# Weight low parts by an accumulating transfer, ten seven-product forms ahead, and two rounds instead of three in the down projection of a trunk layer

## The chip, the cores and the metric

The kernel runs on one core of a Trainium2 chip. The core has five engines with instruction queues of their own: PE (matrix products), DVE and ACT (elementwise work), POOL, and SP, which here issues the transfers between HBM and the on-chip memory. The metric is the device time of one execution in microseconds (us), the median of several runs.

## The reference

One layer works on 128 context tokens and 512 latent tokens (640 together), model width 1024. A mixer stage (mLSTM, convolution, merge, `wo`) comes first. The change lies in the second half, the gated MLP:

```
h2 = rmsnorm(x, p['norm2_g']) * (1 + sc2) + sh2
gate, val = jnp.split(jnp.einsum('btd,df->btf', h2, p['w_up']), 2, axis=-1)
gate = dwconv_grid(gate, p['ffn_dw_w'], p['ffn_dw_b'])      # 3x3 (latent), width 3 (context)
x = x + g2 * jnp.einsum('btf,fd->btd', jax.nn.gelu(gate) * val, p['w_down'])
y = rmsnorm(x, final_norm_g)
```

The inner width is 2816, which is 22 tiles of 128 ("f tiles"). The scale `g2` comes from a linear map of the conditioning vector.

## The kernel before

**Precision.** Every operand of a product is split into a high part and a low part (`hi` is the value rounded to fp32r, `lo` is the value minus `hi`). `three` (line 566) issues three products for each block: high by high, high weight by low data, low weight by high data. So the low part of a weight is read by the third matmul of its block.

**Weights.** All weight blocks of 128x128 stand in HBM in the order in which they are used, eight to a group (512 KB). `load` (436) has SP fetch a group into one of three stage tiles `wst`. `prep` (449) makes `wh` (ACT, a rounding copy) and `wl` (DVE, `tensor_sub` of `wst` and `wh`). There are three `wh` and three `wl` tiles (`NWT`), so `ahead` (518), called when a group begins, prepares the group two places on, whose tiles the group just finished has released.

**The MLP.** `ffn_tile(f)` (1536) computes the gate half of tile f (eight blocks, two column halves of 320 tokens, three products: 48 matmuls) and the value half (another 48). `ffn_gate` copies the gate to `gbuf` on ACT, makes `acc` there, and queues eight taps (`ffn_tap`, DVE). `ffn_out` applies gelu (ACT) and multiplies by the value (DVE, `ge`).

**Rounds.** The down projection of f tiles 0 to 17 is done in three rounds of six f tiles (`ROUNDS`). A round (`dn_round`, 1572) uses a seven-product scheme on 2x2 blocks (token halves by output tiles): in each of four quarters seven products of nine matmuls each, 252 matmuls of 320 columns in place of the 288 of the plain form. Its weights are "forms" (`prep_form`, 470): three are raw blocks (A11, A12, A22), four are sums (S1 to S4, DVE, tile `sf`). Each form gets `hi` (ACT) and `lo` (DVE), both in one `wh` or one `wl` tile, so six forms can be ahead. Its data forms `xf` are made by `pair_forms` (1513) for each pair of f tiles.

Within a quarter the same PSUM bank is read between products: after A11, S2, S3 and so on, `residual` (1338) adds `gate * bank` to the stream `x`, and only then may the next product accumulate into that bank:

```
(pa, "A11", "B11", True, [(m1, 0)]),
(pb, "S1", "T1", True, [(m2, 1)]),
(pa, "S2", "T2", False, [(m1, 1)]),
(pd, "A12", "B21", True, [(m1, 0)]),
(pa, "S3", "T3", False, [(m2, 1)]),
(pb, "S4", "B22", False, [(m1, 1)]),
(pa, "A22", "T4", False, [(m2, 0)]),
```

So DVE must answer A11 while PE does S1, S2 while PE does A12, and S3 while PE does S4.

**The last f tiles.** Tiles 18 to 21 (`LASTF`) are projected in the plain way, once for tokens 0 to 383 (`dnA`) and once for tokens 384 to 639 (`dnB`), with their weight blocks fetched and split for both. For `dnA` the first three output tiles are begun with all but the last f tile. Then `final` scales the result and SP writes it out.

**Order.** Order of issue follows a planner (`_Order`, 167) that keeps estimated times for each engine. DVE's background work waits in `od.bg`: lanes below 20 are taps, lane 20 is the map of the conditioning vector (`ada_tile`, tile `junk`, source tiles `ad`). `step` takes from it while DVE's estimated time stands less than a slack past PE's: `SLACK` for taps, `self.slack` (here `SLACK_FFN`, -1000 ns) for lane 20. `od.need("g2")` in `dn_round` (1572, first round) issues all that is left of the map at that point.

Of the kernel before, what the change touches and what calls it, by code (L numbers as in the profile page):

```python
# [15 lines left out]
P = 128  # L16
# [38 lines left out]

ROUNDS = [list(range(6 * r, 6 * r + 6)) for r in range(3)]
LASTF = list(range(18, NF))
UPS = [list(range(0, 7)), list(range(7, 13)), list(range(13, 19)), list(range(19, NF))]
NPR = 3
# [106 lines left out]
class _Order:  # L166
# [7 lines left out]
    def __init__(self):  # L174
        self.free = {"Q": 1700.0}
        self.ready = {}
        self.side = []
        self.bg = {}
        self.line = None
        self.filling = False  # L180
        self.table = None
        self.hold = False
        self.slack = SLACK
        self.used = {}
        self.rings = {}
        self.avail = {}
# [38 lines left out]
    def issue(self, key, name, ops, args, kw):  # L225
        out, ins = ops[0], ops[1:]
        acc = kw.get("accum_out")
        t = max([self.free.get(key, 0.0)] + [self.ready.get(a.tensor.name, 0.0) for a in ins if a is not acc])
        if key == "Q":
            t = max(t, self.now)  # L230
        t = max(t, self.avail.pop(out.tensor.name, 0.0))
        if key in ("V", "S", "G"):
            t = max(t, self.ready.get(out.tensor.name, 0.0) - self.LAT)
        t += self.cost(key, name, ops, args, kw) * (2 if key == "PE" and t < COLD else 1)
        self.free[key] = t
        done = t + (2000.0 if key == "Q" else self.LAT)
        for a in (out,) if acc is None else (out, acc):
# [57 lines left out]
    def step(self):  # L295
        for t in list(self.side):
            if not t[2] and t[0] <= self.now:
                self._go(t)
        while self.idle_work() and self.free.get("V", 0.0) < self.now + (SLACK if min(self.bg) < 20 else self.slack):
            self.fill()  # L300
# [39 lines left out]
def tile_trunk(  # L340
# [17 lines left out]
    od = _Order()  # L358
    V, S, G, PE, Q = (_Timed(e, od, k) for e, k in ((nc.vector, "V"), (nc.scalar, "S"), (nc.gpsimd, "G"),
                                                    (nc.tensor, "PE"), (nc.sync, "Q")))  # L360

# [17 lines left out]
    ctx.enter_context(tc.manual_schedule())  # L379
    first = ExitStack()  # L380
    adp = first.enter_context(tc.tile_pool(name="adp", bufs=2 * NAD1))
# [67 lines left out]
    def prep(g):  # L449

        if g in ready or g >= NGRP:
            return
        load(g)
        src = stage.pop(g)
        hi = od.ring("wh", wp.tile([P, GB * P], F32R, tag="wh", name="wh"), NWT)
        lo = od.ring("wl", wp.tile([P, GB * P], F32R, tag="wl", name="wl"), NWT)

        def parts():
            yield from od.until(src)
            S.activation(hi, src, AF.Copy)  # L460
            yield
            V.tensor_sub(lo, src, hi.bitcast(F32))
            live.pop(g)

        ready[g] = (hi, lo)
        lines[g] = od.spawn(parts())

    sums_, form_at = {}, {}

    def prep_form(g, j):  # L470
# [9 lines left out]
        a21, a22, a11, a12 = t2[:, 0:FW_], t2[:, FW_:2 * FW_], t1[:, 0:FW_], t1[:, FW_:2 * FW_]  # L480
        tag = ("wh", "wl")[UNIT_AT[u] % 2]
        w = od.ring(tag, wp.tile([P, GB * P], F32R, tag=tag, name=tag), NWT)
        hi, lo = w[:, 0:FW_], w[:, 512:512 + FW_]
        nm = FORMS[j]

        def parts():
# [17 lines left out]
            S.activation(hi, src, AF.Copy)  # L504
            yield
            V.tensor_sub(lo, src, hi.bitcast(F32))
            for gg in (g, g + 1):
# [10 lines left out]
    def ahead(i):  # L518

        room = 2 * NWT  # L520
        while i < len(UNITS):
            kind, g, j = UNITS[i]
            room -= 2 if kind == "c" else 1
            if room < 0:
                break
            if kind == "c":
                prep(g)
# [757 lines left out]
    def close_mid():  # L1285
# [4 lines left out]
        ap2 = ctx.enter_context(tc.tile_pool(name="ap2", bufs=NA2))  # L1290
        adp2 = ctx.enter_context(tc.tile_pool(name="adp2", bufs=NAD))
        ada_cond()
# [180 lines left out]
    def ffn_out(f, pvt):  # L1473
# [11 lines left out]
        if f in LASTF:  # L1485
            hi, lo = A2([P, T], F32R, "ah"), A2([P, T], F32R, "al")
            yield
# [8 lines left out]
    xf, ges, xlive = {}, {}, [0]  # L1496

    def x_form(p, nm, src):

        if xlive[0] < (NA2 if g2_in else NA2 - 4):  # L1500
            t = A2([P, 2, TH], F32R, "xf")
            xlive[0] += 1
            xa2.append(p // 3)
        else:
            t = A([P, 2, TH], F32R, "xf")
        S.activation(t[:, 0, :], src, AF.Copy)
# [46 lines left out]

    od.slack = SLACK_FFN
    first3 = [0, NF, 1]
# [16 lines left out]
    def dn_round(r):  # L1572

        fs = ROUNDS[r]
        for f in fs:
            od.finish(t_act[f])
        if r == 0:
            od.need("g2")
            g2_in.append(True)
        for q in range(4):  # L1580
# [204 lines left out]
```

## Time and profile before

| what | value |
|---|---|
| median of three runs | 1000.87 us (1000.29 to 1001.52) |
| the profiled execution, its own time | 1001.8 us |
| its span | 999.6 us |
| granted TensorE clock, mean | 0.984 |
| busy: PE, DVE, ACT, POOL | 941.7, 803.4, 430.6, 6.0 us |
| HBM read | 105.12 MB |
| MLP begins, up products with h2 | about 489 us |
| last matmul of the down projection | 985 us |

The busy time of an engine says how much of the span it worked. The trace also gives, for each instruction, when it began, and what ended the idle time before it; the latter is what the reading below goes by. Almost every instruction carries the line of the helper that records it (L161 before, L165 after), so tiles tell them apart. A duration of an instruction on DVE or ACT overlaps the next one's beginning a little.

### The profile page before, as it was taken

To read this page: it belongs to the slowest core of one execution; us is meant where nothing else is said; L and a number is where in the kernel's file an instruction comes from. 1 tells how busy PE (TensorE), PEld (TensorE's weight loads), DVE (VectorE), ACT (ScalarE), POOL (GpSimd) and SP (SyncE) were. 2 spreads that over 40 slices of the span, in tenths; PEclk is the share of its full clock that TensorE was granted. 3 is DMA by queue.
4 is the path that set the end of the run, shared out by engine and by line. 5 is a ranking of instruction groups with operands and counts; after the bars stand their busy time and mean duration, and the time that the engine had idled before them with its cause. 6 is when DMAs were issued, how large, how long until landed. Compare 5 with 4: busy or idle time off the path is not lost.

```text
span 999.6 us, 16748 instructions
## 1 busy us (share of the span) xinstructions
PE 941.7 (94%) x6592; PEld 914.4 (91%) x6592; DVE 803.4 (80%) x1600; ACT 430.6 (43%) x836; POOL 6.0 (1%) x41
## 2 busy tenths in 40 slices
PE   5999999999999999999999976999998999989994
PEld 2899999999999999999999975899988999989984
DVE  3858988988888888888878898858789677896667
ACT  4544553367546222245765422333443244333341
POOL 0000000000000000000000000000000000000000
PEclk9999999999999999999999997999999999999997
DMA  9535022211233556575532212322112322124223
GB/s 357 227 101 102 26 75 80 69 54 43 85 127 98 177 181 208 185 267 166 165 106 74 86 47 85 99 87 85 49 35 95 119 64 69 32 69 129 77 70 106
DMA packets 38830, 109.35 MB, mean 109 GB/s; under 512 B 4320, under 2 KB 7264, under 8 KB 38752
## 3 DMA queue, kind: packets, MB, share of 16 engines
q1 hardware_dynamic: 38752, 108.29, 33.8%
q8 instruction: 52, 0.85, 0.3%
q14 instruction: 26, 0.21, 0.1%
HBM read 105.12 MB, written 3.15 MB: 108 GB/s over the span
## 4 chain that ended last, share of the span: by engine, by line
PE 82%; DVE 12%; ACT 3%; issue 2%; DMA 1%; SPq 0%; DVEq 0%
PE mm L161 75%; PE ps L161 8%; DVE x L161 2%; DVE sf L161 2%; DVE wl L161 2%; DVE wh L161 1%; DVE acc L161 1%; DVE junk L161 1%; DVE xf L161 1%; ACT wh L161 1%; DMA x<-in_xT 1%; ACT h L161 0%; ACT L161 0%; DVE sq L161 0%; DVE rsy L161 0%
## 5 line engine op out<-in xcount | busy, mean ns | idle before, releaser
L161 ACT ACTIVATE wh<-wst 128x1024 fp32r<-128x1024 f32 (+1 forms) x138 | 135.5, 983 | 114.5 <-PE mm L161 92.5
L161 DVE SCALAR_TENSOR_TENSOR acc<-gbuf,cols,acc 128x455 f32<-128x455 f32 (+2 forms) x176 | 129.8, 742 | 62.4 <-ACT acc L161 60.2
L161 PE MATMUL mm<-h2h,wh 128*128 128x320 f32 x704 | 165.8, 311 | 0.6 <-ACT h2h L161 0.6
L161 PE MATMUL mm<-h2l,wh 128*128 128x320 f32 x704 | 164.3, 309 | 0.4 <-DVE h2l L161 0.4
L161 PE MATMUL mm<-h2h,wl 128*128 128x320 f32 x704 | 164.5, 309 | 0.0
L161 DVE TENSOR_TENSOR wl<-wst,wh 128x1024 fp32r<-128x1024 f32 x120 | 145.8, 1221 | 21.2 <-ACT wh L161 21.1
L161 PE MATMUL mm<-hh,wh 128*128 128x320 f32 (+2 forms) x576 | 133.8, 311 | 3.5 <-ACT wh L161 2.5
L161 PE MATMUL mm<-hh,wl 128*128 128x320 f32 (+2 forms) x576 | 134.0, 311 | 0.0
L161 PE MATMUL mm<-hl,wh 128*128 128x320 f32 (+2 forms) x576 | 133.4, 311 | 0.0
L161 PEld LDWEIGHTS mm<-h2l,wh 128*128 128x128 f32 x704 | 119.3, 188 | 1.1 <-DVE h2l L161 1.0
L161 PEld LDWEIGHTS mm<-h2h,wh 128*128 128x128 f32 x704 | 118.8, 188 | 1.3 <-ACT h2h L161 1.2
L161 PEld LDWEIGHTS mm<-h2h,wl 128*128 128x128 f32 x704 | 118.4, 188 | 0.1
L161 DVE SCALAR_TENSOR_TENSOR z<-glu,cols,z 128x641 f32<-128x641 f32 (+14 forms) x120 | 102.7, 889 | 4.3 <-ACT z L161 3.5
L161 PEld LDWEIGHTS mm<-hh,wh 128*128 128x128 f32 x576 | 96.3, 188 | 5.5 <-ACT wh L161 3.0
L161 PEld LDWEIGHTS mm<-hl,wh 128*128 128x128 f32 x576 | 96.5, 188 | 2.0 <-issue 1.1
L161 PEld LDWEIGHTS mm<-hh,wl 128*128 128x128 f32 x576 | 96.7, 188 | 1.2 <-issue 0.9
L161 DVE SCALAR_TENSOR_TENSOR junk<-ad,cb 128x512 bf16<-128x512 f32 x128 | 81.7, 686 | 0.0
L161 PE MATMUL mm<-xf,wh 128*128 128x320 f32 x378 | 64.7, 315 | 17.6 <-DVE x L161 17.0
L161 DVE SCALAR_TENSOR_TENSOR x<-mm,mods,x 128x320 f32<-128x320 f32 (+3 forms) x144 | 59.8, 444 | 20.8 <-PE mm L161 20.3
L161 PEld LDWEIGHTS mm<-xf,wh 128*128 128x128 f32 x378 | 58.1, 191 | 19.9 <-ACT wh L161 13.1
L161 PE MATMUL mm<-xf,wl 128*128 128x320 f32 x378 | 65.1, 315 | 10.1 <-DVE x L161 6.0
L161 PEld LDWEIGHTS mm<-xf,wl 128*128 128x128 f32 x378 | 58.0, 191 | 12.8 <-DVE wl L161 5.3
(240 smaller groups left out, 1440.6 us busy)
## 6 DMA issues: line engine op xcount, KB each, us to landing
wst<-in_w SPq DMA_DIRECT2D x120, 512.0 KB, 3.7
ad<-in_ada SPq DMA_DIRECT2D x64, 256.0 KB, 2.9
wst<-in_w SPq DMA_DIRECT2D x24, 384.0 KB, 3.0
adst<-in_ada SPq DMA_DIRECT2D x16, 512.0 KB, 10.4
x<-in_xT SPq DMA_DIRECT2D x16, 320.0 KB, 5.6
out_yT<-x SPq DMA_DIRECT2D x8, 192.0 KB, 2.0
cb<-in_crow SPq DMA_DIRECT2D x4, 256.0 KB, 5.3
out_yT<-yo SPq DMA_DIRECT2D x4, 256.0 KB, 2.2
```

What stands on the lines that cost most here:

```text
L161: return fn(*args, **kw)
```

## The change

Five things change.

1. **Up groups.** For the 40 groups of w_up blocks of f tiles 2 to 21 (`TWICE`), ACT writes `wl` as minus the rounded weight, and POOL issues a transfer that adds the weight from HBM into `wl`. DVE's `tensor_sub` goes. Raw forms (A11, A12, A22) get their low part in the same way. The source stage tile is free once ACT has read it.
2. **Forms ahead.** Four tiles `wf` of 768 columns are added, in the memory of the `ad` tiles, which are closed once the map is done. Forms go round ten places: four `wf`, then `wh` and `wl` in turn.
3. **Two rounds.** f tiles 0 to 11 keep the seven-product scheme. Tiles 12 to 21 are projected plainly, twice, as the last four were.
4. **The map and the taps.** Lane 20 gets `SLACK` in the MLP too, and what is left is issued after up tile 5 at the latest. During a round taps wait for a slack of -3000 ns.
5. **Tiles.** The data parts of the last f tiles are taken from either of two pools (`act_tile`), and the planner counts 6000 ns to landing for the new transfers.

```
-ROUNDS = [list(range(6 * r, 6 * r + 6)) for r in range(3)]
-LASTF = list(range(18, NF))
-UPS = [list(range(0, 7)), list(range(7, 13)), list(range(13, 19)), list(range(19, NF))]
+ROUNDS = [list(range(6 * r, 6 * r + 6)) for r in range(2)]
+LASTF = list(range(12, NF))
+UPS = [list(range(0, 7)), list(range(7, 13)), list(range(13, NF))]
...
+ROUND_SLACK = -3000.0
...
+TWICE = {_g for _g in range(NGRP) if all(nm == "up" and m % NF >= 2 for nm, k, m in BLOCKS[_g * GB:_g * GB + GB])}
+SLOTS = ["wf"] * 4 + ["wh", "wl"] * 3
...
-        if key == "Q":
+        if key in ("Q", "R"):
             t = max(t, self.now)
+        if key == "R":
+            t = max(t, self.ready.get(out.tensor.name, 0.0))
...
-        done = t + (2000.0 if key == "Q" else self.LAT)
+        done = t + {"Q": 2000.0, "R": 6000.0}.get(key, self.LAT)
...
-        while self.idle_work() and self.free.get("V", 0.0) < self.now + (SLACK if min(self.bg) < 20 else self.slack):
+        while self.idle_work() and self.free.get("V", 0.0) < self.now + (self.tap_slack if min(self.bg) < 20 else self.slack):
             self.fill()
...
             S.activation(hi, src, AF.Copy)
+            if g in TWICE:
+                S.activation(lo, src, AF.Copy, scale=-1.0)
+                live.pop(g)
+                GQ.dma_start(lo, w_d[g], accum_op=ALU.add)
+                return
             yield
             V.tensor_sub(lo, src, hi.bitcast(F32))
...
+    wf = []
+    CAPS = {"wh": NWT, "wl": NWT, "wf": 4}
+
+    def slot(u):
+        r, q = PAIRS[u[1]]
+        return SLOTS[(q * len(FORMS) + u[2]) % len(SLOTS)]
...
-        tag = ("wh", "wl")[UNIT_AT[u] % 2]
-        w = od.ring(tag, wp.tile([P, GB * P], F32R, tag=tag, name=tag), NWT)
-        hi, lo = w[:, 0:FW_], w[:, 512:512 + FW_]
+        tag = slot(u)
+        w = od.ring(tag, (wf[0] if tag == "wf" else wp).tile([P, 2 * FW_ if tag == "wf" else GB * P], F32R, tag=tag,
+                                                             name=tag), CAPS[tag])
+        hi, lo = w[:, 0:FW_], w[:, FW_:2 * FW_]
...
             S.activation(hi, src, AF.Copy)
-            yield
-            V.tensor_sub(lo, src, hi.bitcast(F32))
+            if nm[0] == "A":
+                S.activation(lo, src, AF.Copy, scale=-1.0)
+                gg, o = {"A11": (g + 1, 0), "A12": (g + 1, FW_), "A22": (g, FW_)}[nm]
+                GQ.dma_start(lo, w_d[gg, :, o:o + FW_], accum_op=ALU.add)
+            else:
+                yield
+                V.tensor_sub(lo, src, hi.bitcast(F32))
...
-        room = 2 * NWT
+        room = dict(CAPS)
         while i < len(UNITS):
             kind, g, j = UNITS[i]
-            room -= 2 if kind == "c" else 1
-            if room < 0:
+            tags = ("wh", "wl") if kind == "c" else (slot(UNITS[i]),)
+            if any(not room[t] for t in tags) or kind == "f" and not wf:
                 break
+            for t in tags:
+                room[t] -= 1
...
-        adp2 = ctx.enter_context(tc.tile_pool(name="adp2", bufs=NAD))
+        adp2 = last.enter_context(tc.tile_pool(name="adp2", bufs=NAD))
...
-            hi, lo = A2([P, T], F32R, "ah"), A2([P, T], F32R, "al")
+            hi, lo = act_tile([P, T], "ah"), act_tile([P, T], "al")
...
-    od.slack = SLACK_FFN
+    od.slack = SLACK
...
-        if r == 0:
-            od.need("g2")
-            g2_in.append(True)
...
             ffn_tile(f)
+            if not wf and not od.waits("g2") or f == UPS[0][-2]:
+                od.need("g2")
+                if not wf:
+                    g2_in.append(True)
+                    last.close()
+                    wf.append(ctx.enter_context(tc.tile_pool(name="wf", bufs=4)))
         if i < len(ROUNDS):
+            od.tap_slack = ROUND_SLACK
             dn_round(i)
+            od.tap_slack = SLACK
```

Three places show how instructions move.

POOL's queue at the start of the MLP, before (its last rows; the names are `out<-in` with partitions and columns):

```order
L161 MEMSET glu 128x15
L161 MEMSET glu 128x1
L161 MEMSET gbuf_5601 128x656
L161 MEMSET gbuf_5603 128x656
L1772 UNCONDITIONAL_BRANCH
```

and after:

```order
L165 MEMSET gbuf_5601 128x656
L165 MEMSET gbuf_5603 128x656
L165 DMA wl<-in_w 128x1024 x10
L165 DMA wf<-in_w 128x384 x2
L165 DMA wh<-in_w 128x384
L165 DMA wl<-in_w 128x384
L165 DMA wf<-in_w 128x384 x2
```

POOL had nothing to do after clearing `gbuf`; now it issues the accumulating transfers, in the order of use, ten for up groups and then those of raw forms.

DVE's queue at the start of the first round, before. `junk` is the map, `sf` a summed form, `wh<-wst,wh` and `wl<-sf,wl` low parts of forms, and `x<-mm,mods,x` the residuals; the first of them answers product A11:

```order
L161 SCALAR_TENSOR_TENSOR junk,modp<-ad,cb 128x512 x17
L161 TENSOR_TENSOR mods<-modp 128x16
L161 TENSOR_TENSOR mods<-mods,cols 128x16
L161 TENSOR_TENSOR sf<-wst 128x384
L161 TENSOR_TENSOR sf<-wst,sf 128x384
L161 SCALAR_TENSOR_TENSOR x_4894<-mm,mods,x_4894 128x128
L161 SCALAR_TENSOR_TENSOR x_4894<-mm,mods,x_4894 128x192
L161 TENSOR_TENSOR wh<-wst,wh 128x384
L161 SCALAR_TENSOR_TENSOR x_4896<-mm,mods,x_4896 128x320
L161 TENSOR_TENSOR wh<-sf,wh 128x384
L161 SCALAR_TENSOR_TENSOR x_4894<-mm,mods,x_4894 128x320
```

and after, from the last data form on:

```order
L165 TENSOR_TENSOR xf<-tg,xf 128x320
L165 TENSOR_TENSOR sf<-wst 128x384
L165 TENSOR_TENSOR sf<-sf,wst 128x384
L165 SCALAR_TENSOR_TENSOR x_4894<-mm,mods,x_4894 128x128
L165 SCALAR_TENSOR_TENSOR x_4894<-mm,mods,x_4894 128x192
L165 TENSOR_TENSOR wh<-sf,wh 128x384
L165 SCALAR_TENSOR_TENSOR x_4896<-mm,mods,x_4896 128x320
L165 TENSOR_TENSOR sf<-wst 128x384
L165 TENSOR_TENSOR wl<-sf,wl 128x384
L165 SCALAR_TENSOR_TENSOR x_4894<-mm,mods,x_4894 128x320
L165 TENSOR_TENSOR sf<-wst,sf 128x384
L165 TENSOR_TENSOR wf<-sf,wf 128x384
```

The 17 pieces of the map ahead of the first residual are gone from there (they stand between the taps of tiles 0 to 5), and of the low parts only those of summed forms are left.

ACT's queue from the gate of f tile 14 to that tile's gelu, before:

```order
L161 ACTIVATE gbuf_5601<-mm 128x128
L161 ACTIVATE gbuf_5601<-mm 128x3x64
L161 ACTIVATE gbuf_5601<-mm 128x5x64
L161 ACTIVATE acc<-gbuf_5601,cols 128x649
L161 ACTIVATE wh<-wst 128x1024
L161 ACTIVATE xf<-ge 128x320
L161 ACTIVATE xf<-tg 128x320
L161 ACTIVATE xf<-ge 128x320
L161 ACTIVATE xf<-tg 128x320
L161 ACTIVATE wh<-wst 128x1024
L161 ACTIVATE ge<-acc 128x128
L161 ACTIVATE ge<-acc 128x512
```

and after:

```order
L165 ACTIVATE gbuf_5601<-mm 128x128
L165 ACTIVATE gbuf_5601<-mm 128x3x64
L165 ACTIVATE gbuf_5601<-mm 128x5x64
L165 ACTIVATE acc<-gbuf_5601,cols 128x649
L165 ACTIVATE wh<-wst 128x1024
L165 ACTIVATE wl<-wst 128x1024
L165 ACTIVATE wh<-wst 128x1024
L165 ACTIVATE wl<-wst 128x1024
L165 ACTIVATE ge<-acc 128x128
L165 ACTIVATE ge<-acc 128x512
L165 ACTIVATE ah<-ge 128x640
```

Behind each `wh<-wst` stands the negated copy into `wl`, on which POOL's transfer waits; the data forms of the pair are gone, with one `ah` in their place.

More of the change, by code (lines that the diff above doesn't have):

```diff
@@ L182, in __init__ @@
         self.hold = False
-        self.slack = SLACK
+        self.slack = self.tap_slack = SLACK
         self.used = {}
@@ L358, in tile_trunk @@
     od = _Order()
-    V, S, G, PE, Q = (_Timed(e, od, k) for e, k in ((nc.vector, "V"), (nc.scalar, "S"), (nc.gpsimd, "G"),
-                                                    (nc.tensor, "PE"), (nc.sync, "Q")))
+    V, S, G, PE, Q, GQ = (_Timed(e, od, k) for e, k in ((nc.vector, "V"), (nc.scalar, "S"), (nc.gpsimd, "G"),
+                                                        (nc.tensor, "PE"), (nc.sync, "Q"), (nc.gpsimd, "R")))
     cp = ctx.enter_context(tc.tile_pool(name="cp", bufs=1))
@@ L379, in tile_trunk @@
     ctx.enter_context(tc.manual_schedule())
-    first = ExitStack()
+    first, last = ExitStack(), ctx.enter_context(ExitStack())
     adp = first.enter_context(tc.tile_pool(name="adp", bufs=2 * NAD1))
@@ L1496, in tile_trunk, with act_tile @@
     xf, ges, xlive = {}, {}, [0]
-    def x_form(p, nm, src):
[L1500 to L1505, printed above, removed]
+    def act_tile(shape, name, r=None):
+        if xlive[0] < (NA2 if g2_in else NA2 - 4):
+            xlive[0] += 1
+            if r is not None:
+                xa2.append(r)
+            return A2(shape, F32R, name)
+        return A(shape, F32R, name)
+    def x_form(p, nm, src):
+        t = act_tile([P, 2, TH], "xf", p // 3)
         S.activation(t[:, 0, :], src, AF.Copy)
```

## The prediction

> **What bounds the kernel now.** I read the page first, then the timeline of PE, because its gaps and its pace are what the end is made of; then DVE at the gaps.
>
> ```profile
> PE 941.7 (94%) x6592; PEld 914.4 (91%) x6592; DVE 803.4 (80%) x1600; ACT 430.6 (43%) x836; POOL 6.0 (1%) x41
> ...
> 780.00:820.00 40.00, 40.00 (x274) 40.00 (x273) 26.82 (x40) 14.67 (x28) 0.00 (x0) 1.00 0.26 79
> ```
>
> PE is busy 94% of the span. The window is a stretch of up products: PE never stops, DVE has 26.8 of 40 us of work and ACT 14.7. So up tiles are bound by PE, and a faster DVE alone gives nothing there. The timeline of PE shows where it does stop.
>
> ```profile
> 591.61 1.48 PE L161 MATMUL mm<-xf,wh 128*128 128x320 f32 x9
> ...
> 607.28 2.74 PE L161 MATMUL mm<-xf,wh 128*128 128x320 f32 x9 [12.88 <-DVE x L161]
> ...
> L161 PE MATMUL mm<-h2h,wh x480: 303/309/318, 650.2 to 948.7; 128*128 128x320 f32 x160
> ...
> 734.98 1.48 PE L161 MATMUL mm<-xf,wh 128*128 128x320 f32 x9
> ...
> 778.86 0.46 PE L161 MATMUL mm<-h2h,wh 128*128 128x320 f32 x2
> ...
> 863.65 1.48 PE L161 MATMUL mm<-xf,wh 128*128 128x320 f32 x9
> ...
> 907.00 0.45 PE L161 MATMUL mm<-h2h,wh 128*128 128x320 f32 x2
> ```
>
> ```profile
> 600.00:610.00 10.00, 2.71 (x10) 2.75 (x11) 8.46 (x27) 1.66 (x4) 0.00 (x0) 0.50 0.42 122
> ```
>
> Each row is a seven-product form (nine matmuls, `xf`) or the first up matmul behind a round (`h2h`; 650.2 is the first after round 1). The three rounds run from 591.61 to 650.2 (**58.6 us**), from 734.98 to 778.86 (**43.9**) and from 863.65 to 907.00 (**43.35**). Between 650.2 and 734.98 lie six up tiles of 96 matmuls without a gap: 84.8 us, **14.1 us a tile and 0.147 us a matmul**. At that pace a round's 252 matmuls are **37.0 us**, 1.32 us a form. So the rounds lose 21.6, 6.9 and 6.35 us.
>
> In round 1 PE waits 12.88 us for DVE and then does nine matmuls in 2.74 us instead of 1.48; the stretch has a granted clock of 0.50. The timeline of DVE shows what it did meanwhile:
>
> ```profile
> 594.70 0.68 DVE L161 SCALAR_TENSOR_TENSOR junk<-ad,cb 128x512 bf16<-128x512 f32 x1
> ...
> 605.23 0.18 DVE L161 TENSOR_TENSOR mods<-modp 128x16 f32<-128x16 f32 x1
> ...
> 605.53 0.55 DVE L161 TENSOR_TENSOR sf<-wst 128x384 f32<-128x384 f32 x1
> 606.00 0.55 DVE L161 TENSOR_TENSOR sf<-wst,sf 128x384 f32<-128x384 f32 x1
> ```
>
> From 594.70 to 605.23 it does the 17 left pieces of the map (10.5 us); only then come the residuals on which PE waits. The last two rows also show that a 0.55 us instruction is followed by the next after 0.47: successive instructions overlap by 0.08.
>
> In the later rounds DVE is simply full. These are its groups in the window of round 2:
>
> ```profile
> L161 DVE SCALAR_TENSOR_TENSOR x<-mm,mods,x 128x320 f32<-128x320 f32 x16 | 8.8, 548 | 2.3 <-PE mm L161 2.2
> L161 DVE SCALAR_TENSOR_TENSOR x<-mm,mods,x 128x192 f32<-128x192 f32 x11 | 4.5, 408 | 0.0
> ...
> L161 DVE TENSOR_TENSOR sf<-wst 128x384 f32<-128x384 f32 x7 | 3.8, 550 | 0.0
> L161 DVE SCALAR_TENSOR_TENSOR x<-mm,mods,x 128x128 f32<-128x128 f32 x11 | 3.8, 347 | 0.9 <-PE mm L161 0.7
> L161 DVE TENSOR_TENSOR wl<-sf,wl 128x384 fp32r<-128x384 f32 x7 | 3.8, 551 | 0.0
> L161 DVE SCALAR_TENSOR_TENSOR acc<-gbuf,cols,acc 128x455 f32<-128x455 f32 x5 | 3.4, 689 | 0.0
> L161 DVE TENSOR_TENSOR wh<-wst,wh 128x384 fp32r<-128x384 f32 x5 | 2.8, 552 | 0.0
> ```
>
> A quarter of a round has seven residuals, three of them for the first token half (128 and 192 columns, 0.347 + 0.408) and four for the second (0.548): 4.46 us. It has four sums (0.55) and seven low parts (0.55): 6.05. Less 0.08 for each of 21 instructions, that is 8.8 us against 9.25 us of PE, or 35.3 us in a round; taps of the tile ahead (six here, 0.6 each) and some nine instructions for gelu and data forms add 7 us. That makes 42.3, close to the 43.9 that the round takes. So **rounds are bound by DVE, up tiles by PE**.
>
> **The change, part by part.**
>
> *One round less, six f tiles more in the plain tail.* Round 3 goes: -43.35 us. Plain matmuls come twice, with 384 and 256 columns, 24 of each for an f tile: 144 more of each. Their pace:
>
> ```profile
> 949.40 0.34 PE L161 MATMUL mm<-ah,wh 128*128 128x384 f32 x1
> ...
> 953.94 0.34 PE L161 MATMUL mm<-ah,wl 128*128 128x384 f32 x1
> ...
> 957.28 0.52 PE L161 MATMUL mm<-ah,wh 128*128 128x384 f32 x1
> ...
> 960.16 0.47 PE L161 MATMUL mm<-ah,wh 128*128 128x384 f32 x1
> ...
> 976.85 0.28 PE L161 MATMUL mm<-al,wh 128*128 128x256 f32 x1
> 978.71 0.38 PE L161 MATMUL mm<-ah,wl 128*128 128x256 f32 x1 [1.58 <-DVE wl L161]
> ...
> 982.11 0.28 PE L161 MATMUL mm<-ah,wl 128*128 128x256 f32 x1
> ...
> 984.83 0.28 PE L161 MATMUL mm<-ah,wl 128*128 128x256 f32 x1
> ```
>
> The first two rows are 26 matmuls apart: 0.1746 us each. The last two are 24 apart: 0.1133 us. 240 of each cost 69.1 us, the 96 of before 27.6: **+41.5 us**. At PE's pace alone the exchange gains nothing over a round without stalls (37.0 us); it pays because that round cost 43.35.
>
> *The tail's own losses.* From 949.40 to 984.94 before are 35.5 us for 27.6 us of matmuls: 7.9 lost. From 953.94 to 957.28 four matmuls take 3.34 us, since the last f tile's data come late (2.6 lost); the nine up to 960.16 take 0.32 each (1.3 lost); at 978.71 a `wl` is late (1.75); the rest, 2.25, are the sums of squares between. After the change 81 matmuls instead of 27 (14.1 us instead of 4.7) stand before the last f tile is needed, so the first two losses go and the others stay: **4.0 us lost, a gain of 3.9**. The twelve more groups cost ACT 1.05 and DVE 1.2 us each; in `dnB` a group is 24 matmuls, 2.7 us, which leaves DVE about a quarter free beside residuals and squares. What would fill that quarter is the scaling of the first 384 tokens, which now runs beside `dnB` and no longer stands at the very end:
>
> ```profile
> 994.47 1.66 DVE L161 SCALAR_TENSOR_TENSOR x<-x,cols,ps 128x384 f32<-128x384 f32 x3
> ```
>
> Those last three writes took 1.66 us behind the others: **-1.6 us**.
>
> *Round 1.* The map's pieces are no longer ahead of the residuals (the order shows five left behind the taps of tile 5). They cost DVE the same 0.62 us each, hidden in up tiles 0 to 5. What makes room there is the first edit: ten groups lose a `wl` (below, 1.22 us), 12.2 us in all against 10.5 us moved in. From the last h2 data to PE's arrival at 591.61 DVE keeps as much idle time as before, so the last data form is ready about when round 1 begins.
>
> *Low parts of raw forms.* Three of seven go: 3 x (0.55 - 0.08) x 4 = 5.6 us a round, so DVE's 35.3 becomes 29.7; with ten forms instead of six ahead some of that is done before the round; taps, held back, add 3.6 and the rest about 1.6. That is 34.9 us or less against 37.0 of PE. So rounds pass to PE. The turn-round stays: DVE has 1.32 us to answer a product, of which 0.67 is work. Bounds for what is lost to it are 0 and the 6.9 us of round 2; DVE at nine tenths is nearer the free end, and I take **2.5 us a round**: 39.5. That is -19.1 for round 1 and -4.4 for round 2.
>
> *Low parts of up groups.* DVE loses 40 x 1.22 us in stretches that PE bounds: 0. ACT gains 40 x 1.05 us: two more in each 14.1 us tile, on 14.7 of 40: 0, while the chain below holds. The cover is the lead of two groups. The chain now runs on three engines:
>
> ```profile
> 657.29 0.83 ACT L161 ACTIVATE gbuf<-mm 128x128 f32<-128x128 f32 x3 [7.16 <-PE mm L161]
> 658.16 0.93 ACT L161 ACTIVATE acc<-gbuf,cols 128x649 f32<-128x649 f32 x1
> 658.99 1.05 ACT L161 ACTIVATE wh<-wst 128x1024 fp32r<-128x1024 f32 x1
> ```
>
> ```profile
> L161 DVE TENSOR_TENSOR wl<-wst,wh 128x1024 fp32r<-128x1024 f32 x120 | 145.8, 1221 | 21.2 <-ACT wh L161 21.1
> ```
>
> The value half of a tile begins at 657.2. ACT first empties the gate (0.83 + 0.93), then does `wh`, then, new, `wl`, to about 661.0, 3.8 us into the group. The transfer then has until the fourth matmul of the group two places on, 14.7 us after the start: **10.9 us**. In gate halves it is 12.6. The trace has no accumulating transfer and no POOL-issued one. The nearest rows:
>
> ```profile
> DMA  9535022211233556575532212322112322124223
> ...
> wst<-in_w SPq DMA_DIRECT2D x120, 512.0 KB, 3.7
> ...
> wst<-in_w SPq DMA_DIRECT2D x24, 384.0 KB, 3.0
> adst<-in_ada SPq DMA_DIRECT2D x16, 512.0 KB, 10.4
> ```
>
> It moves at least a plain group's bytes, so 3.7 us is the floor; the same bytes took 10.4 at the start of the kernel, where the transfer engines are 9 tenths busy (first digit of the first row). From 384 to 512 KB time grows by 0.7, so 512 KB of movement are 2.8 of the 3.7; reading the target too doubles that: **6.5 us**, nearest to the plain row. That fits in 10.9, and even 10.4 does. Raw forms are a third of the size and have nine forms, 11.9 us, less 1.1 of ACT. Tightest is the second group behind a round: its tiles come free two forms and a group ahead (9.7 us), and with 0.6 for the first four matmuls, less 2.1 of ACT, 8.2 are left. At 6.5 nothing, at 10.4 2.2 us a round. Behind a waiting transfer POOL has only the next transfers, and behind them stands PE's third matmul alone. SP's queue only changes in count; the last three weight loads now stand behind `out_yT` writes, with some 6 us of DVE work between.
>
> *Sum*, against the span of 999.6: -19.1 - 4.4 - 43.35 + 41.5 - 3.9 - 1.6 = -30.9: **968.7**. The execution's own time (1001.8) is 2.2 above its span, so 970.9; the median of runs (1000.87) is 0.9 below that: **970.0**.
>
> **Rivals.**
>
> *The turn-round is missed as often as before.* Then both rounds lose 6.9 as round 2 did, whatever DVE has to do: +8.8, **978.8**. For it: 2.3 us of DVE's own idle time in round 2 were waits for PE on residuals, so it was not always full when PE stood. Against: fewer low parts queue ahead of a residual.
>
> *POOL and DVE hold each other up.* If each of a round's twelve transfers held DVE for one instruction (0.55), 34.9 became 41.5; with the 1.6 us that round 2 took beyond DVE's work, 43.1, or 3.6 more a round: **977.2**. If instead DVE held the transfers, each would wait for its longest instruction, 1.22 us, and 6.5 + 1.22 still fits in 8.2. For it, the trace has no POOL transfer; against, DVE's rows above are all of one kind. The Trainium skill ("SBUF — State Buffer", Who interferes with whom) has this as a rule: GpSimd writes the descriptors of POOL-issued transfers, shares a port pair with DVE, and whoever comes second is blocked for a whole instruction; it advises SP or ACT as issuers. It exempts two-input operations such as those in DVE's rows from blocking GpSimd's writes, so by its letter this rival would not come; no run here shows it yet.
>
> *The transfer is late but not ruinous.* Between 10.9 and 12.4 us a tile loses up to 1.55, 20 tiles up to 31; half of it makes **986**.
>
> *Slower than before.* The gain of 30.9 us over 20 up tiles is 1.55 us a tile, so from 10.9 + 1.55 = **12.4 us** to landing the change loses. At 14 us each tile loses 3.1, 62 us together: about **1032**. So it would if POOL took over 8 us to issue one. Against: that is beyond the slowest row of this size.
>
> *Not what it says.* The order shows the transfers and the shorter DVE list. That no time comes of it would need every stall to have another cause than DVE's queue: 1001.
>
> **How the numbers follow.** Forecast 0.62: 970, by itself from 963 (no stalls in rounds, no late `wl`) to 976. Turn-round 0.16, POOL and DVE 0.05, late transfer 0.07, slower 0.08, nothing 0.02. The range takes in the forecast, the first two rivals and the nearer half of the third: 962 to 985, with some 0.15 left out. A measurement of this kernel tells about 0.2% (2 us) from no change. Faster: 0.62 + 0.16 + 0.05 + 0.07 = 0.90; within: 0.02; slower: 0.08.
>
> **What would show it.** In the profile after: round 1 without a long gap and at full clock, each round 38 to 41 us and PE waiting for `x` only in bits under 1 us; up tiles still 14.1 us with no wait for `wl`; issues of `wl<-in_w` on POOL landing in 5 to 8 us; `dnA` starting without a wait for `al`; both tail paces as above. A wait of PE's third matmul for a transfer in every tile would make it wrong, and so would a DVE busy all through a round.

## The result, and the profile after

The changed kernel takes **966.3 us** (median of 4 runs, 962.98 to 966.47) against 1001.1 before: a ratio of **0.9645, 95% interval 0.9624 to 0.9667**. The forecast was 970.0, the range 962 to 985. The profiled execution has a span of 964.7 us, 34.9 less than before.

First the page (busy time of each engine, share of the span, instructions), then the DMA issues (size of one, median time from issue to landing) and the spread of landings for the tile `wl`, all of the changed kernel:

```profile
PE 939.0 (97%) x6628; PEld 915.6 (95%) x6628; DVE 723.3 (75%) x1437; ACT 469.7 (49%) x869; POOL 61.7 (6%) x105
...
wl<-in_w POOLq DMA_DIRECT2D x40, 512.0 KB, 7.6
wl<-in_w POOLq DMA_DIRECT2D x6, 192.0 KB, 4.8
...
DMA to landing us min/median/max: 3.3/7.4/9.3
```

PE's work is what it was; 32 us of its idle time are gone. The accumulating transfer of 512 KB lands 7.6 us after its issue (median); the slowest into a `wl` tile takes 9.3, inside the cover of 10.9. That is more than the 8.2 us worked out for the second group behind a round, but PE waits for no transfer there. The timeline of PE has the borders of the stages:

```profile
593.13 2.80 PE L165 MATMUL mm<-xf,wf 128*128 128x320 f32 x18
597.01 2.88 PE L165 MATMUL mm<-xf,wf 128*128 128x320 f32 x18 [1.08 <-DVE x L165]
...
631.80 0.46 PE L165 MATMUL mm<-h2h,wh 128*128 128x320 f32 x2
...
716.60 0.60 PE L165 MATMUL mm<-xf,wf 128*128 128x320 f32 x3
...
754.93 0.45 PE L165 MATMUL mm<-h2h,wh 128*128 128x320 f32 x2
...
882.13 0.34 PE L165 MATMUL mm<-ah,wh 128*128 128x384 f32 x1
...
953.06 0.28 PE L165 MATMUL mm<-ah,wl 128*128 128x256 f32 x1
```

The rounds take 631.80 - 593.13 = **38.7 us** and 754.93 - 716.60 = **38.3**; the wait of 12.9 us in round 1 has become one of 1.08. Six up tiles still take 84.8, nine 127.2. The waits of PE between 500 us and the end (us in all, times, longest) name all that is left:

```profile
PE ps L165 <- DVE rsy L165: 2.0, 1, 2.0
PE mm L165 <- DVE x L165: 1.1, 1, 1.1
PE ps L165 <- ACT sq L165: 0.8, 1, 0.8
PE mm L165 <- ACT wf L165: 0.7, 1, 0.7
PE mm L165 <- ACT h2h L165: 0.5, 1, 0.5
PE mm L165 <- DVE h2l L165: 0.4, 2, 0.2
PE mm L165 <- DMA wl<-in_w: 0.2, 1, 0.2
```

One wait of 0.2 us for a transfer is all, and it is for the first of them, at 522.96. The rounds keep a wait of 1.08 us for `x`, a little more than the "bits under 1 us" of the prediction. The windows of both rounds and of the tail (length; then busy PE, weight loads, DVE, ACT, POOL; granted clock; DMA share; GB/s):

```profile
593.13:631.80 38.67, 37.59 (x254) 36.97 (x253) 33.08 (x75) 18.44 (x35) 9.08 (x11) 1.00 0.67 148
716.60:754.93 38.33, 37.60 (x254) 36.95 (x253) 30.53 (x70) 19.41 (x36) 8.68 (x10) 1.00 0.68 148
...
882.13:953.17 71.04, 71.04 (x506) 70.34 (x504) 44.82 (x72) 28.17 (x38) 0.00 (x0) 1.00 0.43 138
```

PE is busy 37.6 of 38.3 to 38.7 us, DVE 30.5 to 33.1 instead of 40. The prediction's terms beside what the two traces show:

| term, us | forecast | measured |
|---|---|---|
| start of round 1 | 0 | +1.5 |
| round 1 | -19.1 | -19.9 |
| round 2 | -4.4 | -5.6 |
| round 3 | -43.35 | -43.35 |
| six f tiles more in the tail, with its losses (41.5 - 3.9) | +37.6 | +35.5 |
| from the last matmul on a weight to the end | -1.6 | -3.1 |
| sum | -30.9 | -34.9 |

The start of round 1 lies between 590.0 and 593.4 us in all the runs below, at 593.15 without any transfer (run 7) and at 591.50 with all of them (run 8). Of the 1.5 us here, 1.05 stand already at the first up matmul (488.94 us before, 489.99 after), ahead of all that the change touches. The other 0.5 come with the wait for the first transfer and the slower matmuls behind it; runs 3, 6 and 9 show that wait too, the others don't.

### The profile page after: what moved, and what is told of

The parts are those of the page before. It is cut to its first block, busy times and chain, and to the rows that moved or that the text cites. A ratio compares the mean times of both kernels' runs of the same rounds, so it can differ in the third digit from the quotient of the medians.

```text
span 964.7 us, 16850 instructions
## 1 busy us (share of the span) xinstructions
PE 939.0 (97%) x6628; PEld 915.6 (95%) x6628; DVE 723.3 (75%) x1437; ACT 469.7 (49%) x869; POOL 61.7 (6%) x105
## 4 chain that ended last, share of the span: by engine, by line
PE 92%; ACT 3%; DVE 3%; DMA 1%; issue 1%; SPq 0%; DVEq 0%
PE mm L165 84%; PE ps L165 8%; DMA wl<-in_w 1%; DVE acc L165 1%; ACT wh L165 1%; DMA x<-in_xT 1%; ACT wf L165 0%; ACT h L165 0%; DVE yo L165 0%; DVE junk L165 0%; ACT L165 0%; ACT h2h L165 0%; DVE rsy L165 0%; DVE xf L165 0%; ACT sq L165 0%
## 5 line engine op out<-in xcount | busy, mean ns | idle before, releaser
L165 ACT ACTIVATE wh<-wst 128x1024 fp32r<-128x1024 f32 (+1 forms) x144 | 144.3, 1007 | 112.8 <-PE mm L165 87.2
L165 DVE TENSOR_TENSOR wl<-wst,wh 128x1024 fp32r<-128x1024 f32 x92 | 111.9, 1221 | 30.7 <-ACT wh L165 30.4
L165 DVE SCALAR_TENSOR_TENSOR x<-mm,mods,x 128x128 f32<-128x128 f32 (+2 forms) x104 | 43.2, 443 | 22.1 <-PE mm L165 21.9
L165 POOL DMA_DIRECT2D wl<-in_w x46 | 40.1, 871 | 279.3 <-ACT wl L165 168.1
L165 ACT ACTIVATE wl<-wst 128x1024 fp32r<-128x1024 f32 (+1 forms) x52 | 47.4, 922 | 3.8 <-PE mm L165 3.8
L165 PE MATMUL mm<-ah,wh 128*128 128x384 f32 (+1 forms) x160 | 49.2, 307 | 0.0
L165 PE MATMUL mm<-ah,wl 128*128 128x384 f32 (+1 forms) x160 | 49.1, 307 | 0.0
```

The lines of the kernel that those rows point to most:

```text
L165: return fn(*args, **kw)
```

## The experiments

Twelve kernels. The kernel before was run beside each set; its medians were 1001.6 to 1002.2, so kernels are compared by ratios to it. 0.001 is 1 us, and differences under some 2.7 us between two of these kernels can't be told from none. Round times are from PE's timeline in the one profiled execution.

| run | ratio to before, 95% | us against the changed kernel | round 1 | round 2 |
|---|---|---|---|---|
| changed kernel | 0.9645 (0.9624 to 0.9667) | 0 | 38.7 | 38.3 |
| 1 up low parts on DVE | 0.9713 (0.9694 to 0.9732) | +6.8 | 45.8 | 39.1 |
| 2 raw low parts on DVE | 0.9700 (0.9686 to 0.9715) | +5.5 | 41.3 | 41.8 |
| 3 taps not held | 0.9658 (0.9642 to 0.9674) | +1.3 | 41.4 | 38.2 |
| 4 six forms ahead | 0.9893 (0.9879 to 0.9908) | +24.8 | 43.9 | 45.3 |
| 5 three rounds | 0.9682 (0.9665 to 0.9699) | +3.7 | 38.7 | 38.4 |
| 6 tail by transfer | 0.9867 (0.9847 to 0.9886) | +22.2 | 38.7 | 38.3 |
| 7 no transfer | 0.9763 (0.9748 to 0.9777) | +11.8 | 46.0 | 44.4 |
| 8 eight forms ahead | 0.9662 (0.9648 to 0.9677) | +1.7 | 39.2 | 39.2 |
| 9 six ahead, raw on DVE | 0.9809 (0.9778 to 0.9841) | +16.4 | 41.5 | 41.1 |
| 10 plain transfers | 0.9634 (0.9618 to 0.9651) | -1.1 | 38.7 | 38.3 |
| 11 before, map moved | 0.9893 (0.9875 to 0.9910) | +24.8 | 48.0 | 43.9 |
| 12 six ahead, plan of 4 us | 0.9825 (0.9788 to 0.9863) | +18.0 | 42.3 | 41.6 |

### What each kind of transfer is worth: runs 1, 2 and 7

```
-TWICE = {_g for _g in range(NGRP) if all(nm == "up" and m % NF >= 2 for nm, k, m in BLOCKS[_g * GB:_g * GB + GB])}
+TWICE = set()
```

> The changed kernel, but the low parts of the 40 up groups are subtracted on DVE again (no transfers for them); raw forms keep theirs. Theory of the prediction: up tiles stay bound by PE, but the 12.2 us of DVE work (ten groups at 1.22) that made room for the map's 10.5 us come back ahead of round 1, so the last data form or the map is late there: round 1 begins 5 to 10 us later or has a gap of that size, rounds 1 and 2 themselves stay near 38.5, total 971 to 977 us against 966.3. Rival A: DVE had 16 us idle in the 100 us ahead of round 1 anyway, so the room was there and the time is the same within 2 us. Rival B: the transfers cost something that is not seen (the first rows of h2 come 1.0 us later after the change than before): then this kernel is 1 us or more faster than the changed one.

It took 973.83 us. This is the first theory: up tiles stayed at 14.1 us, and the loss is a wait in round 1 (PE's timeline):

```profile
599.94 5.14 PE L165 MATMUL mm<-xf,wf 128*128 128x320 f32 x18 [5.68 <-DVE x L165]
604.88 0.47 PE L165 MATMUL mm<-xf,wh 128*128 128x320 f32 x1
```

Behind a wait of 5.68 us instead of 1.08, 18 matmuls took 4.94 us (604.88 - 599.94) and not 2.7: 4.6 + 2.2 of the 7.1 by which round 1 is longer. Round 2 lost only 0.8.

```
-            if nm[0] == "A":
+            if nm == "-":
                 S.activation(lo, src, AF.Copy, scale=-1.0)
```

> The changed kernel, but the low parts of the raw forms (three of seven) are subtracted on DVE again; up groups keep their transfers, the lead stays ten forms. Theory of the prediction: 12 x 0.47 = 5.6 us of DVE come back in each round, 34.9 becomes 40.5 against 37.0 of PE, so each round takes 2 to 4 us longer (40.5 to 42.5) and the total is 970 to 974. Rival: the lead of ten forms and the taps held back already carry it, rounds stay at 38.3 to 39.2 and the total within 1.5 us of 966.3.

972.05 us, with rounds of 41.3 and 41.8: each lost some 3, in the middle of the expected 2 to 4. Together they hold six waits for `x`, 5.7 us, where the changed kernel has one of 1.08 (and one of 0.66 for `wf`). But DVE is not full, as the expectation had it (40.5 us). The window of the first round:

```profile
593.13:634.47 41.34, 38.61 (x254) 37.00 (x253) 33.20 (x77) 15.16 (x25) 1.72 (x2) 1.00 0.35 95
```

DVE is busy 33.2 us, as in the changed kernel's round 1 (33.1), mostly because two taps run in it instead of seven. So the size was right, and the sum of DVE's work that gave it was not: it is low parts in front of residuals that PE waits for, while DVE as a whole has time left.

Run 7 has both edits:

> The changed kernel without any accumulating transfer: low parts of up groups and of raw forms are subtracted on DVE; lead of ten, two rounds, map and taps as changed. Theory: the two effects are of different places (12.2 us of DVE ahead of round 1: +6.8; low parts inside rounds: +5.5) and add: 978 to 980. Rival A: they share DVE's queue in round 1, so more than the sum: 982 to 990. Rival B: the transfers themselves cost something that goes with them: less than the sum, 974 or below.

978.09 us: the totals add (6.8 + 5.5 = 12.3 against 11.8). The rounds do not: round 1 lost 7.3 us where the single losses make 9.8, round 2 lost 6.1 where they make 4.2. So the sum is right and the separation of places is not.

### Where the taps stand: run 3

```
-            od.tap_slack = ROUND_SLACK
```

> The changed kernel, but taps are not held back in a round (the planner's slack for them stays 450 instead of -3000). Theory: some six taps of 0.6 to 0.7 us stand ahead of residuals in each round, with 1.32 us to answer a product and 0.67 us of it work, so a tap in the way costs PE up to 0.6 us: rounds 1 to 3 us longer each, total 968 to 972. Rival: DVE is off the path in rounds now, so their place is of no account: within 1 us of 966.3.

968.18 us, 1.3 more, which can't be told from none. In the profile round 1 is 2.8 us longer and round 2 not at all:

```profile
598.51 4.12 PE L165 MATMUL mm<-xf,wf 128*128 128x320 f32 x18 [2.32 <-DVE x L165]
602.43 1.81 PE L165 MATMUL mm<-xf,wh 128*128 128x320 f32 x9
```

Two taps of 0.70 us (594.61, 595.61) stand between the last data forms, and the first residual comes 4.3 us after the round's first product (597.70 - 593.39); in the changed kernel it comes after 3.1 (596.19 - 593.13). In round 2 it comes 2.1 us after, with taps about it too (721.68 - 719.63). So holding the taps back counts where DVE comes late to a round. That it is the map that makes it late in round 1 is likely and was not tested alone.

### The number of rounds: run 5

```
-ROUNDS = [list(range(6 * r, 6 * r + 6)) for r in range(2)]
-LASTF = list(range(12, NF))
-UPS = [list(range(0, 7)), list(range(7, 13)), list(range(13, NF))]
+ROUNDS = [list(range(6 * r, 6 * r + 6)) for r in range(3)]
+LASTF = list(range(18, NF))
+UPS = [list(range(0, 7)), list(range(7, 13)), list(range(13, 19)), list(range(19, NF))]
```

> The changed kernel with three rounds of six f tiles and four plain ones, as before the change; transfers, lead of ten, map and taps as changed. Theory: a round now takes 38.4 us against 41.5 us of plain matmuls for the same six tiles, -3.1; but the tail of four tiles loses again what it lost before (last f tile's data late 3.9, sums of squares 2.2, against 1.8 now: up to +4.3) and the end gets its scaling back (14.7 against 11.5: +3.1): in sum +2 to +5, total 968 to 972 against 966.3. Rival A: tail and end gained through DVE's freed time and not through the number of plain tiles; then they stay and this kernel is faster, about 963. Rival B: exchange of a round is where the gain was: 970 to 980 with the third round at 41 us or more.

971.08 us, as the theory had it. The third round and the tail, in PE's timeline:

```profile
840.06 0.60 PE L165 MATMUL mm<-xf,wf 128*128 128x320 f32 x3
...
878.39 0.46 PE L165 MATMUL mm<-h2h,wh 128*128 128x320 f32 x2
...
920.78 0.34 PE L165 MATMUL mm<-ah,wh 128*128 128x384 f32 x1
...
926.74 0.44 PE L165 MATMUL mm<-ah,wh 128*128 128x384 f32 x1 [1.07 <-ACT ah L165]
928.11 0.64 PE L165 MATMUL mm<-al,wh 128*128 128x384 f32 x1 [0.93 <-DVE al L165]
...
950.03 0.38 PE L165 MATMUL mm<-ah,wl 128*128 128x256 f32 x1 [1.60 <-DVE wl L165]
```

The third round takes 38.3 us too, 3.1 less than its six tiles cost as plain ones. But the tail of four tiles with the end takes 970.9 - 920.8 = 50.1 us, the 50.2 of before, with the same three waits. So what tail and end gained in the changed kernel comes from the number of plain tiles, not from DVE's freed time; and with the new rounds the exchange is still worth 3.7 us by the medians (5.9 in the two profiled executions: 38.3 + 50.1 - 82.6, the last being tail and end of the changed kernel).

### How much cover a transfer needs, and what makes it long: runs 6 and 10

```
-TWICE = {_g for _g in range(NGRP) if all(nm == "up" and m % NF >= 2 for nm, k, m in BLOCKS[_g * GB:_g * GB + GB])}
+TWICE = {_g for _g in range(NGRP) if all(nm == "up" and m % NF >= 2 or nm in ("dnA", "dnB") for nm, k, m in BLOCKS[_g * GB:_g * GB + GB])}
```

> The changed kernel, with the low parts of the 20 groups of the plain tail (dnA, dnB) also by accumulating transfer. Theory (the cover rule of the prediction): from a tile coming free to its low part: two ACT copies of 1.05, then 7.6 us to landing, 9.7 us, and the tile is wanted two groups and some 0.4 us later; a dnA group is 24 x 0.1746 = 4.2 us, a dnB group 2.7, so groups are slowed to about 4.7 us each: +5 us in dnA, +20 in dnB, total about 991 (984 to 996), PE waiting for wl by DMA. Rival: 7.6 us is queue time that shrinks when transfers follow each other, then no loss, and with DVE free of 1.2 us a group the tail gains up to 2: 964 to 966.

988.9 us. PE's waits in the tail:

```profile
PE mm L165 <- DMA wl<-in_w: 15.8, 11, 4.7
```

and two of them in the timeline:

```profile
890.70 0.45 PE L165 MATMUL mm<-ah,wl 128*128 128x384 f32 x1 [0.54 <-DMA wl<-in_w]
895.58 0.45 PE L165 MATMUL mm<-ah,wl 128*128 128x384 f32 x1 [0.40 <-DMA wl<-in_w]
```

These two groups of `dnA` are 4.9 us apart, not 4.2, and tail and end together take 23.3 us longer (25 expected); 15.8 of it are the waits. This is the mechanism of the prediction's slower rival in another place: the same transfer that costs next to nothing in groups of 7 us costs 22 us where a group lasts 4.2 and 2.7.

```
-GQ.dma_start(lo, w_d[g], accum_op=ALU.add)
+GQ.dma_start(lo, w_d[g])
```

> The changed kernel, but the 40 transfers for up groups write the weights over the tile and don't add to it; queue, size, place and the two ACT copies are the same. It leaves out the subtraction of the high parts, so the low parts of the up weights are the whole weights. Theory (estimate of the prediction: reading the target too is what makes it long): landing falls from 7.6 to about 4.1, that of SP's plain load of 512 KB; total the same within 1 us, since nothing waits for it. Rival: the queue of POOL, not the adding, is slow: landing stays at 7 us or more.

966.01 us, the same. Its DMA issues, and POOL's instructions for the tile `wl` (min/median/max in ns), first of this run:

```profile
wst<-in_w SPq DMA_DIRECT2D x132, 512.0 KB, 3.7
wl<-in_w POOLq DMA_DIRECT2D x40, 512.0 KB, 4.6
...
L165 POOL DMA_DIRECT2D wl<-in_w x46: 527/528/915, 513.1 to 862.8; - x46
```

then of the changed kernel:

```profile
L165 POOL DMA_DIRECT2D wl<-in_w x46: 865/865/1007, 514.8 to 865.0; - x46
```

It is the adding that takes 3.0 of the 7.6 us, and 0.34 of POOL's 0.87 us per issue; issued by POOL, a plain transfer is 0.9 us slower than SP's load of the same size in this run (3.7). The Trainium skill ("DMA: Bandwidth & Descriptors", Anatomy of one DMA — SWDGE (gpsimd) path) has a fit for transfers issued by GpSimd, 2.0 us plus the bytes at 436 GB/s; for 512 KB that is an estimate of 3.2 us. The plain transfer took 1.4 more here, the accumulating one 4.4 more, and it is the measured ones that count.

### The map alone: run 11

In the kernel before:

```
-    od.slack = SLACK_FFN
+    od.slack = SLACK
...
             ffn_tile(f)
+            if f == UPS[0][-2]:
+                od.need("g2")
```

> The kernel before, but with the map's left pieces done among the up tiles ahead of round 1 (due by f tile 5) instead of in round 1; all else as before. Theory of the prediction: the gap of 12.9 us and the half clock go, but DVE had 12.8 us idle in the 80 us ahead of round 1 and gets 10.5 more to do, in the wrong places: a wait of 2 to 8 us is left at the start of round 1, which is otherwise like round 2 (43.9): 989 to 995 us against 1001.8. Rival A: the room for it came from the transfers alone, so the wait only moves to the head of round 1: 996 to 1001. Rival B: there was room anyway: 986 to 988.

991.18 us, 10.7 less than before and inside the expected 989 to 995. Round 1 goes from 58.6 to 48.0, with this wait (PE's timeline):

```profile
597.99 2.47 PE L161 MATMUL mm<-xf,wh 128*128 128x320 f32 x8 [4.01 <-DVE x L161]
```

The round is 4.1 us longer than round 2 (43.9), so beside the wait it is like round 2, as expected. Moving the map gave 10.6 of round 1's 19.9 us. Of the other 9.3, 7.3 come with the transfers (46.0 in run 7 against 38.7) and 2.0 with the rest of the change.

### The lead of ten: runs 4, 8, 9 and 12

```
-SLOTS = ["wf"] * 4 + ["wh", "wl"] * 3
+SLOTS = ["wh", "wl"] * 3
```

> The changed kernel, but forms use the six tiles of before (three wh, three wl) and not the four more: six forms ahead instead of ten. Theory: the transfer of a raw form lands 5 us after its issue and has five forms, 6.6 us, less 1.1 us of ACT, so it is in time; but four forms less are built before the round, two sums and two low parts or so (2 us of DVE) move into it: rounds 1 to 2.5 us longer, total 968 to 971. Rival A: the lead is not needed, within 1 us of 966.3. Rival B: transfers are late with six, PE waits for low parts by DMA in most quarters: over 975.

991.92 us: rival B's total, but not by its waits, and far beyond the theory. The windows of its two rounds and of the stretch behind the first:

```profile
592.85:636.78 43.93, 38.28 (x255) 36.98 (x253) 33.53 (x76) 22.49 (x43) 10.46 (x12) 1.00 0.61 136
728.62:773.90 45.28, 39.34 (x255) 38.38 (x253) 31.80 (x72) 22.44 (x42) 10.44 (x12) 0.96 0.61 135
...
636.78:650.00 13.22, 8.93 (x45) 8.67 (x44) 0.68 (x2) 1.06 (x1) 0.86 (x1) 0.74 0.84 206
```

and rows of PE's timeline in the round and behind it, then of DVE's in the round:

```profile
607.70 1.56 PE L165 MATMUL mm<-xf,wl 128*128 128x320 f32 x9 [2.82 <-ACT ge L165]
...
609.10 1.48 PE L165 MATMUL mm<-xf,wh 128*128 128x320 f32 x9
...
641.81 0.90 PE L165 MATMUL mm<-h2h,wl 128*128 128x320 f32 x2 [4.29 <-DMA wl<-in_w]
642.51 0.74 PE L165 MATMUL mm<-h2h,wh 128*128 128x320 f32 x2
...
647.31 0.50 PE L165 MATMUL mm<-h2h,wh 128*128 128x320 f32 x2
```

```profile
604.35 0.69 DVE L165 SCALAR_TENSOR_TENSOR acc<-gbuf,cols,acc 128x455 f32<-128x455 f32 x1
605.08 0.56 DVE L165 TENSOR_TENSOR wh<-sf,wh 128x384 fp32r<-128x384 f32 x1
605.55 1.41 DVE L165 SCALAR_TENSOR_TENSOR acc<-gbuf,cols,acc 128x455 f32<-128x455 f32 x2
606.88 1.13 DVE L165 SCALAR_TENSOR_TENSOR x<-mm,mods,x 128x128 f32<-128x128 f32 x3
```

Two losses. *Behind a round* the first up group's transfer is 4.3 us late: with six places its tiles come free only as the last forms are used. With the lower clock after it (0.74) the stretch takes 91.8 us instead of 84.8. *In a round* DVE is busy only 32 to 34 of 44 to 45 us and PE loses as much as before the change, when DVE was full: three taps (0.69, and two in 1.41) stand ahead of the residuals of 606.88. PE starts when the first of them are done, at 607.70; `ge`, which the row names, ends just then too, but PE doesn't read it. Not every wait has taps ahead of it: the 1.57 us that end at 629.99 follow a sum (627.41), its copy on ACT and its low part (628.69), for which DVE itself waits 0.73 us. Two things are open: how many forms are enough, and why the taps stand there.

```
-SLOTS = ["wf"] * 4 + ["wh", "wl"] * 3
+SLOTS = ["wf"] * 2 + ["wh", "wl"] * 3
...
-    CAPS = {"wh": NWT, "wl": NWT, "wf": 4}
+    CAPS = {"wh": NWT, "wl": NWT, "wf": 2}
...
-                    wf.append(ctx.enter_context(tc.tile_pool(name="wf", bufs=4)))
+                    wf.append(ctx.enter_context(tc.tile_pool(name="wf", bufs=2)))
```

> The changed kernel with two more tiles for forms instead of four: eight forms ahead. With six the rounds took 43.9 and 45.3 us and the up groups behind a round waited 6 to 7 us for their transfers, 25 us in all. Theory (lead by dose): each tile of lead takes some of both, rounds at 40 to 42, some 1 to 3 us behind each round, total 974 to 984. Rival A (threshold): what matters is that the round trip sum (DVE), copy (ACT), low part (DVE) of a form is no longer placed right ahead of a residual; two tiles more do that, total within 3 us of 966.3. Rival B: only the ring's free tiles behind a round count: rounds at 38 to 39, losses only behind them.

968.03 us, 1.7 more, not to be told from none: a threshold, not a dose. Rounds take 39.2 each, and one wait of 0.3 is all that is seen of the transfers behind them.

> The changed kernel with six forms ahead (as in the fourth run) and the raw forms' low parts on DVE: no raw transfer is left, up groups keep theirs. With six ahead and raw transfers it took 991.9 us (ratio to before 0.9893). Theory A (lead): with six ahead each quarter has a sum, its ACT copy and its low part in one row on DVE ahead of a residual; taking the raw transfers away changes nothing in that and DVE gets 5.6 us a round back, so rounds take 44 us or more, total 990 to 998. Theory B (short transfers): a raw transfer of 4 to 5 us is too late for a lead of five forms less the ACT copies (5.5 us) and that made the rounds 43.9 and 45.3; then without them rounds are back at about 41.5, as with a lead of ten and low parts on DVE, total 983 to 987.

982.73 us; this has the edits of runs 2 and 4. Rounds of 41.5 and 41.1 are those of run 2 with ten ahead (41.3, 41.8). So with raw low parts made on DVE the lead doesn't change the rounds. With six ahead it is the raw transfers that lengthen them, by their own time or by what the planner makes of it; the last run tells these apart in part. The window of its first round shows more work on DVE than in run 4 and a shorter round:

```profile
591.69:633.16 41.47, 38.23 (x255) 36.97 (x253) 35.27 (x81) 17.27 (x29) 1.73 (x2) 1.00 0.32 99
```

The losses behind the rounds are still 5.4 us each; they belong to the up groups' transfers.

```
-done = t + {"Q": 2000.0, "R": 6000.0}.get(key, self.LAT)
+done = t + {"Q": 2000.0, "R": 6000.0 if self._size(out) > 512 else 4000.0}.get(key, self.LAT)
```

> The changed kernel with six forms ahead, raw forms by transfer, as in the fourth run; only the planner's assumption for a raw transfer is 4 us instead of 6 (it is 6 for both sizes in the change; raw transfers were measured at 3.8 to 4.5 us there, up groups at 7.5). Theory A (plan): with six ahead a transfer taken for 6 us doesn't fit in the 6.6 us of five forms less two copies, so the planner believes PE late and puts taps, gelu products and low parts ahead of residuals, and it is these that PE really waits for; with 4 us they move behind, rounds fall from 43.9 and 45.3 to 39 to 41, the losses behind the rounds (6 to 7 each) stay: total 979 to 985 against 991.9. Theory B (the transfer itself is late): rounds stay at 43 or more, total 989 to 993.

985.03 us (interval of the ratio 0.9788 to 0.9863, clear of run 4's): the total is at the upper end of what the first theory gave, the rounds (42.3 and 41.6) fall between the two theories. The planner's 6 us are part of it, 1.6 and 3.7 us of the rounds. DVE's rows at the place of run 4's wait of 2.82 us:

```profile
602.27 0.69 DVE L165 SCALAR_TENSOR_TENSOR acc<-gbuf,cols,acc 128x455 f32<-128x455 f32 x1
602.88 1.13 DVE L165 SCALAR_TENSOR_TENSOR x<-mm,mods,x 128x128 f32<-128x128 f32 x3
```

One tap stands ahead of these residuals instead of three, and PE's wait is 1.62 us. A planner's figure nearer the measured one (4.6 us here) helped. The rest of the gap, down to the 39.2 of eight ahead, was not taken apart further.

## Why the prediction was right

- **Rounds pass from DVE to PE.** Right in its result: 38.7 and 38.3 us at full clock. 2.5 us a round were set down for the missed turn-round; 1.7 and 1.3 it was. DVE does 33.1 and 30.5 us, not 34.9. The rival (missed as often as before) falls with lead ten. But the reason was too simple: that DVE is "simply full" is not what a round's loss hangs on. In run 4 it was about three quarters busy and the rounds lost 7 to 8 us, in run 2 it did hardly more than in the changed kernel's round 1 and they lost 4 to 5, by what stood ahead of a residual. So that a DVE sum of 34.9 against 37.0 of PE came out as a free round is in part luck. The prediction gave the lead a small part, some work done before the round; without raw transfers it gave nothing (runs 2 and 9), and with them six were too few (runs 4 and 12) and eight enough (run 8).
- **Round 1 and the map.** Right: the gap is gone. That the `wl` taken from DVE makes the room is shown from both sides: without it PE waits 5.7 us (run 1), and with the move alone 4.0 (run 11). The move itself was worth about half.
- **Up groups' low parts cost nothing.** Right but for some 0.5 us at the first transfer, with 7.6 us to landing where 6.5 was the estimate. That the adding is what makes the transfer long is shown: 3.0 us (run 10) against the 2.8 worked out for reading the target. That it is this reading which takes the 3.0 is not shown. The cover rule held where it was tested in other places: by its number in the tail (run 6, 23.3 us against 25), by its sign behind a round with six ahead (run 4).
- **POOL and DVE don't hold each other up.** The groups of DVE in a stretch of up tiles, first after the change, where POOL issues a transfer per group (x, busy, mean ns):

```profile
L165 DVE SCALAR_TENSOR_TENSOR acc<-gbuf,cols,acc 128x455 f32<-128x455 f32 (+2 forms) x24 | 17.9, 744 | 13.0 <-ACT acc L165 12.3
L165 DVE TENSOR_TENSOR ge<-ge,mm 128x320 f32<-128x320 f32 x6 | 2.7, 484 | 5.0 <-ACT ge L165 5.0
```

  then before it:

```profile
L161 DVE SCALAR_TENSOR_TENSOR acc<-gbuf,cols,acc 128x455 f32<-128x455 f32 (+2 forms) x24 | 17.8, 742 | 11.9 <-ACT acc L161 11.5
...
L161 DVE TENSOR_TENSOR ge<-ge,mm 128x320 f32<-128x320 f32 x6 | 2.7, 484 | 2.1 <-ACT ge L161 2.1
```

  744 against 742 ns, and 484 both times. Nor does DVE hold POOL: its issues take 0.865 us at the least and 1.007 at the most. The Trainium skill's exemption of two-input operations ("SBUF — State Buffer", Who interferes with whom) agrees with the `acc` rows, whose operation reads both `gbuf` and `acc`; `ge` reads its other input from PSUM.
- **One round for six plain tiles.** Right in sign, 3.6 us too small: -43.35 + 35.5 - 3.1 = -10.95 where -7.35 was worked out (-43.35 + 37.6 - 1.6). Of the tail's losses, "the others stay" failed: the late `wl` of `dnB` went too, and with four tiles it is there in spite of the transfers (1.60 us in run 5). The likely reason is that ten f tiles put 30 matmuls between a residual and the next instead of 12. The end gained 3.1 us and not 1.6: the last three writes gave some 1.4, and the sums of squares, no longer behind DVE's scaling, 0.8. Another 0.9 is luck, as far as the runs tell: the last broadcast took PE 1.07 us instead of 1.94 in this execution, and 1.90 and 1.94 in those of runs 4 and 8, which have the same tail.
- **All parts together.** Against before, the map's place gives 10.7 us (run 11); with the exchange, the lead and the taps it is 23.7 (run 7); the transfers give the other 11.8. No variant was faster than the changed kernel by more than can be measured.

## What to carry to other kernels

A transfer that adds in flight takes work off a compute engine at no cost as long as the time from issue to landing, with the copies ahead of it, fits between the moment its buffer comes free and its first use; where groups get shorter, or the ring of buffers smaller, the same transfer turns into the bound. A share of busy time of 75% doesn't say that an engine is off the path: in a loop that hands products to and fro, look at what stands directly ahead of the instruction that is waited for. And the time that a planner assumes for a transfer shapes the order of other engines: take it from a trace.

## What the runs showed of the hardware that was not expected

Adding costs a transfer of 512 KB 3.0 us more than writing (7.6 against 4.6), and POOL 0.34 us more per issue. Waits can cost more than their length: behind one of 4.29 us, pairs of matmuls took 0.53 us instead of 0.29 (642.51 to 647.31 in run 4), another 2.7 us in all; the granted clock is 0.50 from 641.81 to 647.31. In run 3, 18 matmuls behind a wait of 2.32 us took 3.92 us at a granted clock of 0.66, and in run 4's second round nine behind 2.53 us took 2.54 at 0.50. But in its first round nine behind 2.82 us took 1.40 at 1.00. What decides between them is open; the length of the wait alone doesn't.
